# Encoder block on one core: q/k rows in another order, rotary low parts on VectorE, splits at the ends of projections, entry squares on two engines

## The chip, the cores and the metric

One NeuronCore of a Trainium2 chip runs the kernel. It has five engines that run their own instruction lists and wait for each other by semaphores: TensorE (PE in the profile, with PEld for its weight loads), VectorE (DVE), ScalarE (ACT), GpSimd (POOL) and SyncE (SP), which only issues DMA transfers here. DMAs issued by SP, ACT and POOL run on queues of their own. The metric is the device time of one execution in microseconds, the median of several runs.

## What is computed

One encoder block in float32 on an input x of 1024 positions by 1024 features:

```python
h = rms_norm(x, attn_pre_gain[l])
proj = h @ w_in[l]                      # 1024 x 3072
u_hy = proj[..., :3 * HYENA_WIDTH]      # x0, x1, v of the Hyena group, 512 each
q, k, v = jnp.split(proj[..., 3 * HYENA_WIDTH:], 3, axis=-1)
h_fwd, h_bwd = implicit_filters(...)    # small MLP with sines, times a decay window
y_hy = hyena_mixer(u_hy, ...)           # short conv of 3 taps; long conv of v*x1 by FFT; times x0
q = apply_rope(q.reshape(B, S, ATTN_HEADS, 2, ATTN_HEAD_DIM), cos, sin) * scale
k = apply_rope(k.reshape(B, S, ATTN_HEADS, 2, ATTN_HEAD_DIM), cos, sin)
o = differential_attention(q, k, v, lam)   # 4 heads, two softmax maps each, w = p0 - lam * p1
o = rms_norm(o, subln_gain[l], SUBLN_EPS) * (1.0 - lam_init)
mix = jnp.concatenate([y_hy, y_attn], axis=-1) @ w_out[l]
x = x + rms_norm(mix, attn_post_gain[l])
h = rms_norm(x, mlp_pre_gain[l])
y = jnp.square(jax.nn.relu(h @ w_up[l])) @ w_down[l]
x = x + rms_norm(y, mlp_post_gain[l])
```

## The kernel before

**High and low parts.** Every matmul operand is split into a rounded high part (type fp32r) and the rest, its low part, and a product is three matmuls: high by high, high by low, low by high. ACT writes the high part (`act`, a copy), and `less` subtracts it from the full value on POOL ("P") or DVE ("V"), at line L146. `tt` is a tensor_tensor on either of these two engines (L361).

**Buffers.** SBUF tiles come from tagged rings: A 32, B 12, W 6, T 8 and U 6 tiles of 4 KB a partition. A new tile of a tag waits until the oldest one's last reader, a store included, is done. PSUM has banks for single tiles (`bank`) and two double ones for the projections (`bank2`).

**Order of the work, up to the attention.**
- *Entry.* Eight tiles x0 to x7 are loaded. Of the first four, ACT squares each with an accumulated row sum (`square`, L268), `normalize` makes the reciprocal root (L128 to L136) for tiles 0 and 1, for 2, and for 3, and DVE scales them (`xn`, L273). PE transposes them (`n1t`, L278), ACT and DVE make hT's high and low parts (L281, L282), and the projections begin (`pj`, L251).
- *Projections* of 128 columns take 48 matmuls of 512 columns. Those of x1 and v of the Hyena group come first, with a three-tap convolution (`short_conv`, L334 on ACT, L336 on DVE).
- *Filter spectrum*, in two halves of 256 channels (`filter_spectrum`): PE makes `hsp` (L497, L498), DVE multiplies by the decay table `dec` to `hst` (L501), ACT and POOL or DVE split it (`hsd`, L505 and L146; the string EHS names the engines in turn), PE transforms it (L355), and `eight` adds and subtracts the transforms (EWG names the engine of each of nine steps) and stores them to `gd` (L520).
- *The q/k stage.* `todo` has four pairs: (t, pr) with t = 0 for q, 1 for k. A pair has 256 raw columns, 4 heads' parts of 64; it is turned into two streams z = 0, 1 (first and second halves of the rotary dimension), each 128 columns, so `pjqk101` is t = 1, pr = 0, z = 1. `pair_raw` loads, `pair_split` splits, `stream` runs the 48 matmuls. `rotary_a` (after the first stream) makes ac and as, `rotary_b` (after the second) makes bs and bc, adds them to the two turned halves, splits them (ACT and POOL), and stores four tiles of 512 KB to `qk` (L748, two from ACT's queue and two from POOL's).
- *Beside it*, DVE works off `turn_uv` and two `conv_unit`s: the DFT of v times x1 (tiles b0u to b7u, L355), sums and differences (sdeu, ev1u, sdou, opu, nxu, exu), products with the filter spectrum (`unit_product`: loads G0u and G1u, t2, abu, dfu, pq0u, pq1u) and stores. These are generators: `stream` and `vector` keep two estimated times, PE's and DVE's, and a piece of a unit is placed in the order whenever DVE's estimate lies behind PE's.
- *x0.* Four more streams (pj0 to pj3) with their short convolutions, then v, then the attention: scores `s`, DVE's row maximum `nm` (L955), ACT's exponential, and so on. Output projection and MLP follow.

The order is written out by hand (manual scheduling) on all engines in these stages. The pair's columns of high and low weights stand head first, then place in the rotary half:

```python
raws.append(raw.rearrange("p k (g z j) -> p z (k g) j", z=2, j=32))
...
hv, lv = (x[:, 4 * kh:4 * kh + 4, :].rearrange("p k (g j) -> p (k g) j", j=32) for x in (hi, lo))
```

so a tile's 128 rows are 4 heads by 32 places, and the store's outer dimension is (h c), 4.

## Time and profile before

| | us |
|---|---|
| median of 3 runs (lowest, highest) | 1296.97 (1296.13, 1297.72) |
| the profiled execution, its own time | 1294.01 |
| its span, first to last instruction | 1292.2 |
| PE busy | 1217.1 (94%) |
| DVE busy | 1014.6 (79%) |
| ACT busy | 534.5 (41%) |
| POOL busy | 221.3 (17%) |
| mean granted clock of TensorE | 0.982 |

The granted clock is a share of full speed, 2.4 GHz; 0.50 is TensorE's other level, 1.2 GHz. Engines work side by side, so busy shares don't add. An instruction's idle time in square brackets is the time that its engine stood before it, and behind the arrow is what let it go.

### The profile page before, as it was taken

To read this page: it belongs to the slowest core of one execution; us is meant where nothing else is said; L and a number is where in the kernel's file an instruction comes from. 1 tells how busy PE (TensorE), PEld (TensorE's weight loads), DVE (VectorE), ACT (ScalarE), POOL (GpSimd) and SP (SyncE) were. 2 spreads that over 40 slices of the span, in tenths; PEclk is the share of its full clock that TensorE was granted. 3 is DMA by queue.
4 is the path that set the end of the run, shared out by engine and by line. 5 is a ranking of instruction groups with operands and counts; after the bars stand their busy time and mean duration, and the time that the engine had idled before them with its cause. 6 is when DMAs were issued, how large, how long until landed. Compare 5 with 4: busy or idle time off the path is not lost.

```text
span 1292.2 us, 16582 instructions
## 1 busy us (share of the span) xinstructions
PE 1217.1 (94%) x6064; PEld 1018.6 (79%) x6064; DVE 1014.6 (79%) x1698; ACT 534.5 (41%) x1040; POOL 221.3 (17%) x229
## 2 busy tenths in 40 slices
PE   6999899779999999899998999999999999999985
PEld 4787588668989898788886888888887888888873
DVE  5756889897866999956799766687778889887887
ACT  5423231122166777633454323233235544444433
POOL 1233224335131265200100000011110000000000
PEclk9999799889999999999999999999999999999997
DMA  8230424555875342123622432434580704354043
GB/s 253 52 108 16 163 99 131 149 174 186 239 162 123 109 128 68 58 98 101 201 91 74 147 129 91 152 125 157 196 322 10 291 21 162 146 196 163 1 146 115
DMA packets 109720, 172.85 MB, mean 134 GB/s; under 512 B 24587, under 2 KB 71750, under 8 KB 109638
## 3 DMA queue, kind: packets, MB, share of 16 engines
q1 hardware_dynamic: 79334, 125.31, 29.4%
q0 software_dynamic: 29248, 42.28, 11.5%
q10 hardware_dynamic: 1056, 4.19, 1.0%
q8 instruction: 48, 0.79, 0.2%
q14 instruction: 34, 0.28, 0.1%
HBM read 121.10 MB, written 50.33 MB: 133 GB/s over the span
## 4 chain that ended last, share of the span: by engine, by line
PE 68%; DVE 16%; issue 7%; DMA 5%; ACT 2%; POOL 1%; ACTq 0%; DVEq 0%; SPq 0%; POOLq 0%
PE dx L1517 11%; PE pj L251 10%; PE ux L1356 9%; PE mix L1068 7%; PE dz L1517 6%; PE uz L1356 4%; PE s L949 4%; PE o L995 3%; PE dy L1517 3%; PE uy L1356 2%; PE wtp L980 2%; DMA qk<-as 2%; PE v L806 2%; DMA wv_raw<-in_w_in_dram 1%; DVE nm L955 1%
## 5 line engine op out<-in xcount | busy, mean ns | idle before, releaser
L251 PE MATMUL pj<-hT,wi_hi 128*128 128x512 f32 x384 | 124.0, 402 | 0.3 <-DVE hT L282 0.3
L955 DVE TENSOR_REDUCE nm<-s 128x1 f32<-128x1024 f32 x64 | 77.4, 1215 | 31.5 <-PE s L949 31.4
L1517 PE MATMUL dx<-dpT,dpS 128*128 128x512 f32 x384 | 89.2, 390 | 3.7 <-ACT dpT L1500 2.6
L1068 PE MATMUL mix<-wo,yc 128*128 128x512 f32 x384 | 89.8, 392 | 0.0
L251 PE MATMUL pjqk<-hT,wq_hi 128*128 128x512 f32 x256 | 81.7, 401 | 7.4 <-DVE as L697 6.9
L1517 PEld LDWEIGHTS dx<-dpT,dpS 128*128 128x128 f32 x384 | 71.9, 188 | 19.7 <-ACT dpT L1500 3.0
L957 ACT ACTIVATE p<-s,nm 128x1024 f32<-128x1024 f32 x64 | 71.4, 1117 | 38.3 <-DVE nm L955 18.6
L251 PEld LDWEIGHTS pj<-hT,wi_hi 128*128 128x128 f32 x384 | 72.2, 192 | 16.6 <-issue 1.9
L1068 PEld LDWEIGHTS mix<-wo,yc 128*128 128x128 f32 x384 | 71.4, 188 | 14.4
L251 PE MATMUL pj<-hT,wi_lo 128*128 128x512 f32 x192 | 76.7, 400 | 1.2 <-POOL wi_lo L146 1.2
L995 PEld LDWEIGHTS o<-v,wt 128*128 128x128 f32 x512 | 62.1, 191 | 2.6
L995 PE MATMUL o<-v,wt 128*128 128x128 f32 x512 | 62.2, 275 | 0.0
L251 PEld LDWEIGHTS pjqk<-hT,wq_hi 128*128 128x128 f32 x256 | 48.2, 193 | 17.8 <-issue 8.5
L1517 PE MATMUL dx<-dpT,dpA 128*128 128x512 f32 x192 | 48.2, 407 | 4.8 <-ACT dpT L1500 4.1
L251 PE MATMUL pjqk<-hT,wq_lo 128*128 128x512 f32 x128 | 50.8, 397 | 0.0
L1517 PEld LDWEIGHTS dx<-dpT,dpA 128*128 128x128 f32 x192 | 37.2, 195 | 15.4 <-ACT dpT L1500 5.6
L1517 PE MATMUL dy<-dpB,dpA 128*128 128x512 f32 x192 | 46.7, 401 | 2.1 <-ACT dpB L1500 1.5
L1500 ACT ACTIVATE dpA<-dg 128x512 fp32r<-128x512 f32 x48 | 30.1, 628 | 44.5 <-PE dx L1517 26.8
L146 DVE TENSOR_TENSOR wS<-wur,wS 128x512 fp32r<-128x512 f32 x64 | 43.6, 686 | 5.0 <-ACT wS L1349 4.9
L806 PE MATMUL v<-wv_hi,hT 128*128 128x256 f32 x256 | 47.0, 284 | 0.0
L949 PE MATMUL s<-stK,stQ 128*128 128x512 f32 x128 | 42.6, 413 | 4.2 <-ACT p L957 4.2
L1349 ACT ACTIVATE wS<-wur 128x512 fp32r<-128x512 f32 x64 | 37.5, 625 | 21.7 <-DVE wur L1343 15.0
(424 smaller groups left out, 3108.5 us busy)
## 6 DMA issues: line engine op xcount, KB each, us to landing
wur<-in_w_up_dram SPq DMA_DIRECT2D x32, 512.0 KB
dg<-gu SPq DMA_DIRECT2D x32, 512.0 KB
dw<-in_w_down_dram SPq DMA_DIRECT2D x32, 512.0 KB
gu<-gb POOLq DMA_DIRECT2D x16, 512.0 KB, 2.9
wi_raw<-in_w_in_dram SPq DMA_DIRECT2D x12, 512.0 KB
dS<-gs SPq DMA_DIRECT2D x24, 256.0 KB
gu<-ga POOLq DMA_DIRECT2D x10, 512.0 KB, 3.7
x<-in_x_dram SPq DMA_DIRECT2D x8, 512.0 KB
```

The lines of the kernel that those rows point to most:

```text
L146: (G if eng == "P" else V).tensor_tensor(out=out, in0=in_, in1=f32(hi), op=ALU.subtract)
L251: mm(out=pj[c][:, hf * 512:hf * 512 + 512], lhsT=w[:, k, :], rhs=hT[k][s][hf], start=(k == 0 and n == 0), stop=(k == KT - 1 and n == 2))
L806: mm(out=pt[:, col:col + 256], lhsT=hT[k][s][hf][:, q0:q0 + P], rhs=ws[k // 4][o][:, k % 4, :], start=(n == 0), stop=(n == 3 * KT - 1))
L949: mm(out=soft["s", n][e][:, ks], lhsT=stacks[hd, "Q", e][:, qs], rhs=stacks[hd, part, e][:, ks], start=(z == 0), stop=(z == 1))
L955: V.tensor_reduce(out=nmax[:, e:e + 1], in_=soft["s", n][e], axis=AX.X, op=ALU.max, negate=True)
L957: act(out=pc, in_=soft["s", n][e], func=AF.Exp, bias=nmax[:, e:e + 1], accum_out=soft[hd, "r0"][:, qt:qt + 1] if e == 0 else soft["r", n][ ...
L995: mm(out=soft["ov", h][:, i * P:(i + 1) * P], lhsT=wt[:, k // 4, (k % 4) * P:(k % 4) * P + P], rhs=vv[hd // 2, k // 4][:, k % 4, (hd % 2) ...
L1068: mm(out=mixed[i][:, sl], lhsT=ycat[c][hf][s][:, q0:q0 + P], rhs=wo[c][o][:, sl], start=(c == 0 and n == 0), stop=(c == 7 and n == 2))
L1349: act(out=hi, in_=block(p, OVER[n]), func=AF.Copy)
L1356: mm(out=out, lhsT=w[s_][:, k, :], rhs=x[o][k], start=(m in (1, 2, 5) and k == 0 and n == 0), stop=(k == 3 and n == 2), skip_group_check=m ...
L1500: act(out=t[:, 0, :], in_=blk[p, nm], func=AF.Copy)
L1517: mm(out=down_bank(c, m, tp), lhsT=g[s_][:, tp * P:tp * P + P], rhs=w[o], start=(m in (1, 2, 5) and j == 0 and n == 0), stop=(j == PC - 1 ...
```

## The change

- `hsd`'s low parts and all nine steps of `eight` are on DVE (EHS, EWG).
- The gain vector's load moves from SP's queue to POOL's.
- A pair's columns are ordered place first, then head: `pair_split` writes with a step of four elements, the rotary table repeats each place four times, and the stores have an outer dimension of 32.
- In `rotary_b`, both adds come first, then the two low parts on DVE; ACT copies both high parts before it issues its two stores. The planner counts six operations of 1024 columns there, not four.
- The next pair's (or x0's) split stands at the end of the stream; raw weights of x0 are loaded up to two streams ahead.
- At the entry, the second square is a product and a sum on DVE, one normalisation serves four tiles, the fourth tile is scaled by ACT, and the gain columns are made before it.
- The first decay table of a half takes a buffer of tag U. In `conv_unit`, `fetch(1)` and `fetch(3)` come later, filters are loaded one at a time at four places, and ny reuses the tile oc.

```diff
@@ -33,8 +33,8 @@
 
 CONV_LAG = 8.0
 
-EHS = "PV"
-EWG = ("VPPVVVVVV", "PPVVVVVVV")
+EHS = "V"
+EWG = ("VVVVVVVVV", "VVVVVVVVV")
 EWU = ("V" * 9, "V" * 9)
 EUV = "VPVPVPVV"
 ELV = "PP"
@@ -168,7 +168,7 @@
     rows = slot("B", [64, P], F32, "rows")
     V.memset(rows, 0.0)
     gain = slot("B", [8, P], F32, "gain")
-    nc.sync.dma_start(out=gain, in_=a["attn_pre_gain"].rearrange("o (k p) -> (o k) p", p=P))
+    nc.gpsimd.dma_start(out=gain, in_=a["attn_pre_gain"].rearrange("o (k p) -> (o k) p", p=P))
 
     def load_rows():
         nc.sync.dma_start(out=rows[8:44], in_=a["conv_w"].rearrange("o w (k p) -> (o w k) p", p=P))
@@ -228,7 +228,7 @@
         for kh in range(2):
             raw = slot("W", [P, 4, 256], F32, f"wq{t}{pr}{kh}_raw")
             nc.sync.dma_start(out=raw, in_=a["w_in"][0].rearrange("(k p) n -> p k n", p=P)[:, 4 * kh:4 * kh + 4, c0:c0 + 256])
-            raws.append(raw.rearrange("p k (g z j) -> p z (k g) j", z=2, j=32))
+            raws.append(raw.rearrange("p k (g z j) -> p z k g j", z=2, j=32))
         return raws
 
     def pair_split(raws, t, pr, z):
@@ -236,7 +236,7 @@
         hi = slot("W", [P, KT, P], F32R, f"wq{t}{pr}{z}_hi")
         lo = slot("W", [P, KT, P], F32R, f"wq{t}{pr}{z}_lo")
         for kh in range(2):
-            hv, lv = (x[:, 4 * kh:4 * kh + 4, :].rearrange("p k (g j) -> p (k g) j", j=32) for x in (hi, lo))
+            hv, lv = (x[:, 4 * kh:4 * kh + 4, :].rearrange("p k (j g) -> p k g j", g=4) for x in (hi, lo))
             act(out=hv, in_=raws[kh][:, z], func=AF.Copy)
             less("P", lv, raws[kh][:, z], hv)
         wcols["qk", t, pr, z] = hi, lo
@@ -267,9 +267,18 @@
         xn[i] = slot("U" if i < 4 else "B", [P, D], F32, f"xn{i}")
         act(out=xn[i], in_=xs[i], func=AF.Square, accum_out=ssq[:, i:i + 1])
 
-    def normalize(i0, n):
+    def square_v(i):
+
+        xn[i] = slot("U", [P, D], F32, f"xn{i}")
+        V.tensor_tensor(out=xn[i], in0=xs[i], in1=xs[i], op=ALU.mult)
+        V.tensor_reduce(out=ssq[:, i:i + 1], in_=xn[i], axis=AX.X, op=ALU.add)
+
+    def normalize(i0, n, on_act=()):
         r = mean_rstd(ssq[:, i0:i0 + n], n, f"n1_{i0}")
         for i in range(n):
+            if i in on_act:
+                act(out=xn[i0 + i], in_=xs[i0 + i], func=AF.Copy, scale=r[:, i:i + 1])
+                continue
             V.tensor_scalar(out=xn[i0 + i], in0=xs[i0 + i], scalar1=r[:, i:i + 1], scalar2=None, op0=ALU.mult)
 
     def norm1_t(hf, k):
@@ -289,11 +298,12 @@
             load_x(i)
         for c in (5, 9):
             raws[c] = col_raw(a["w_in"][0], c, f"wi{c}", "B")
-        for i0, n in ((0, 2), (2, 1), (3, 1)):
-            for i in range(n):
-                square(i0 + i)
-            normalize(i0, n)
+        square(0)
+        square_v(1)
+        square(2)
+        square(3)
         load_cols(gain, gcols)
+        normalize(0, 4, (3,))
         wcols[4] = col_split(raws[4], "wi4")
         for k in range(KT):
             norm1_t(0, k)
@@ -483,7 +493,7 @@
 
         dec = []
         for i in range(2):
-            t = slot("T", [P, 4, 256], F32, f"dec{hf}_{i}")
+            t = slot("UT"[i], [P, 4, 256], F32, f"dec{hf}_{i}")
             nc.sync.dma_start(out=t, in_=a["c_decay"][4 * i:4 * i + 4, :, hf * 256:hf * 256 + 256].rearrange("t p c -> p t c"))
             dec.append(t)
         fb = slot("T", [1, 256], F32, f"fb{hf}")
@@ -544,13 +554,11 @@
-        def filters(kt):
...
+        gs = {}
+
+        def filters(kt, m):
+            g = gs[kt, m] = slot("T", [P, 2, 2, 256], F32, f"G{m}{nm}{kt}")
+            nc.sync.dma_start(out=g.rearrange("p s c n -> p s (c n)"), in_=g_dram[hf][2 * kt + m])
...
-        fetch(1)
...
+        fetch(1)
         fetch(7, "co")
-        fetch(3)
-        dft_done[0] = hf
...
+            if n == 1 and w == 0:
+                fetch(3)
...
-        gs = filters(0)
+        for m in range(2):
+            filters(0, m)
...
-        gs = filters(1)
...
-        ny = pairs(f"ny{nm}")
+        ny = oc
...
+        if filters:
+            filters(1, 0)
...
@@ -646,6 +656,8 @@
             V.tensor_tensor(out=pq[m][:, 0, :], in0=t[:, 0, :], in1=t[:, 1, :], op=ALU.add)
             yield T512
             V.tensor_tensor(out=pq[m][:, 1, :], in0=t[:, 0, :], in1=t[:, 1, :], op=ALU.subtract)
+            if filters and m == 0:
+                filters(1, 1)
             nc.sync.dma_start(out=q_dram[u][m], in_=pq[m])
             yield T512
 
@@ -738,48 +750,49 @@
         bs, bc = (slot("U", [P, L], F32, f"b{x}{nm}") for x in "sc")
         turned_by(t, bs, pb, rope[1])
         turned_by(t, bc, pb, rope[0])
-        vector(4 * T1024)
-        for z, (x_, y_, op) in enumerate(((ac, bs, SUB), (bc, as_, ADD))):
+        vector(6 * T1024)
+        both = ((ac, bs, SUB), (bc, as_, ADD))
+        for x_, y_, op in both:
             tt("V", x_, x_, y_, op)
+            act(out=y_.bitcast(F32R), in_=x_, func=AF.Copy)
+        for z, (x_, y_, op) in enumerate(both):
             hi, lo = y_.bitcast(F32R), x_.bitcast(F32R)
-            act(out=hi, in_=x_, func=AF.Copy)
-            tt("P", lo, x_, y_, SUB)
+            tt("V", lo, x_, y_, SUB)
             for s_, half in enumerate((hi, lo)):
                 (nc.scalar, nc.gpsimd)[s_].dma_start(
-                    out=qk_dram[t][2 * pr:2 * pr + 2, :, s_, 32 * z:32 * z + 32, :].rearrange("h c j l -> (h c) j l"), in_=f32(half))
+                    out=qk_dram[t][2 * pr:2 * pr + 2, :, s_, 32 * z:32 * z + 32, :].rearrange("h c j l -> j (h c) l"), in_=f32(half))
 
     with tc.manual_schedule(engines=MAN):
         beside += [turn_uv(), conv_unit(0, uv), conv_unit(1, uv)]
         todo = [(t, pr) for pr in range(2) for t in range(2)]
         raws = {todo[0]: pair_raw(*todo[0])}
-        pair_split(raws[todo[0]], *todo[0], 0)
-
-        def next_raw(n):
-            if n < 4:
-                raws[todo[n]] = pair_raw(*todo[n])
-            else:
-                raws[0] = col_raw(a["w_in"][0], 0, "wi0")
-
-        def next_split(n):
-            if n < 4:
-                pair_split(raws[todo[n]], *todo[n], 0)
-            else:
-                wcols[0] = col_split(raws[0], "wi0")
-
-        pair_split(raws[todo[0]], *todo[0], 1)
-        for n, (t, pr) in enumerate(todo):
-            pa = stream(("qk", t, pr, 0), {0: [lambda: next_raw(n + 1)]})
-            ab_ = rotary_a(t, pr, pa)
-            pb = stream(("qk", t, pr, 1), {6: [lambda: next_split(n + 1)]})
-            if n + 1 < 4:
-                pair_split(raws[todo[n + 1]], *todo[n + 1], 1)
-            rotary_b(t, pr, pb, *ab_)
-
-        def x0_next(c):
-            wcols[c] = col_split(col_raw(a["w_in"][0], c, f"wi{c}"), f"wi{c}")
-
+        for z in range(2):
+            pair_split(raws[todo[0]], *todo[0], z)
+
+        def x0_raw(c):
+            raws[c] = col_raw(a["w_in"][0], c, f"wi{c}")
+
+        def x0_split(c):
+            wcols[c] = col_split(raws[c], f"wi{c}")
+
+        for n, u in enumerate(todo):
+            more = todo[n + 1:n + 2]
+            pa = stream(("qk", *u, 0), {0: [lambda: raws.update({w: pair_raw(*w) for w in more}) if more else x0_raw(0)]})
+            for w in more:
+                pair_split(raws[w], *w, 0)
+            if not more:
+                x0_split(0)
+            ab_ = rotary_a(*u, pa)
+            pb = stream(("qk", *u, 1), {} if more else {2: [lambda: x0_raw(1)]})
+            for w in more:
+                pair_split(raws[w], *w, 1)
+            if not more:
+                x0_split(1)
+            rotary_b(*u, pb, *ab_)
         for c in range(4):
-            stream(c, {4: [lambda: x0_next(c + 1)]} if c < 3 else {})
+            stream(c, {2: [lambda: x0_raw(c + 2)]} if c < 2 else {})
+            if c in (0, 1):
+                x0_split(c + 2)
             o = short_conv(c, "U", f"x0_{c}")
             vector(3.0)
             nc.sync.dma_start(out=x0_dram[c], in_=o)
@@ -1777,7 +1790,7 @@
     invf = (f4(10000.0) ** (-np.arange(0, DH, 2, dtype=f4) / f4(DH))).astype(f4)
     ang = (np.arange(L, dtype=f4)[:, None] * invf[None, :]).astype(f4)[tau].T
     co, si = np.cos(ang), np.sin(ang)
-    rope = np.stack([np.concatenate([co] * 4), np.concatenate([si] * 4)]).astype(f4)
+    rope = np.stack([np.repeat(co, 4, axis=0), np.repeat(si, 4, axis=0)]).astype(f4)
     return {"c_fwd": fwd.reshape(4, P, 1024), "c_inv": inv.reshape(4, P, 512), "c_z": zt,
             "c_decay": dec, "c_rope": rope}
 
```

The order moves at three places that matter below. On DVE around the third pair of q/k (`ac01` and `as01` belong to its first stream, `bs10` to the second pair's second), before:

```order
L699 TENSOR_TENSOR bs10_1845<-pjqk101_1768,rope1_1406 128x1024
L699 TENSOR_TENSOR bc10_1846<-pjqk101_1768,rope0_1405 128x1024
L361 TENSOR_TENSOR ac10_1764<-ac10_1764,bs10_1845 128x1024
L361 TENSOR_TENSOR bc10_1846<-bc10_1846,as10_1765 128x1024
...
L634 TENSOR_TENSOR abu00_1903<-nxu0_1762,exu0_1661 128x512
L636 TENSOR_TENSOR abu00_1903<-exu0_1661,nxu0_1762 128x512
L638 TENSOR_TENSOR dfu00_1904<-nxu0_1762,exu0_1661 128x512
...
L646 TENSOR_TENSOR pq0u00_1922<-abu00_1903 128x512
L697 SCALAR_TENSOR_TENSOR ac01_1925<-pjqk010_1863,rope0_1405 128x1024
L697 SCALAR_TENSOR_TENSOR as01_1926<-pjqk010_1863,rope1_1406 128x1024
```

and after the change:

```order
L711 TENSOR_TENSOR bs10_1825<-pjqk101_1756,rope1_1391 128x1024
L711 TENSOR_TENSOR bc10_1826<-pjqk101_1756,rope0_1390 128x1024
L371 TENSOR_TENSOR ac10_1752<-ac10_1752,bs10_1825 128x1024
L371 TENSOR_TENSOR bc10_1826<-bc10_1826,as10_1753 128x1024
L371 TENSOR_TENSOR ac10_1752<-ac10_1752,bs10_1825 128x1024
L371 TENSOR_TENSOR bc10_1826<-bc10_1826,as10_1753 128x1024
...
L709 SCALAR_TENSOR_TENSOR ac01_1904<-pjqk010_1843,rope0_1390 128x1024
L709 SCALAR_TENSOR_TENSOR as01_1905<-pjqk010_1843,rope1_1391 128x1024
L635 TENSOR_TENSOR exu0_1639<-exu0_1639,t21u00_1884 128x2x256
L637 TENSOR_TENSOR exu0_1639<-exu0_1639,t21u00_1884 128x2x256
L644 TENSOR_TENSOR abu00_1934<-nxu0_1779,exu0_1639 128x512
```

The two low parts (the second L371 of ac10 and of bc10) are new on DVE, and the reads of the third pair's first stream now stand ahead of abu, dfu and pq0u. On PE, the first DFT tile of unit 1, b4u1, before:

```order
L251 MATMUL pjqk111_2091<-hT5_1_1_387,wq111_hi_2007 128x512
L251 MATMUL pjqk111_2091<-hT5_1_0_386,wq111_lo_2008 128x512
L355 MATMUL b4u1_2154<-uv0_0_1395,fw2_669 128x256
L355 MATMUL b4u1_2154<-uv0_1_1396,fw2_669 128x256
```

and after the change:

```order
L251 MATMUL pj1_2221<-hT0_1_1_314,wi1_hi_2131 128x512
L251 MATMUL pj1_2221<-hT0_1_0_313,wi1_lo_2133 128x512
L365 MATMUL b4u1_2256<-uv0_0_1380,fw2_654 128x256
L365 MATMUL b4u1_2256<-uv0_1_1381,fw2_654 128x256
```

It stood behind 42 of the 48 matmuls of the last q/k stream; now it stands behind that stream, the whole of pj0 and 27 of pj1. On DVE around the first row maximum of the attention (`nm0_0`), before:

```order
L646 TENSOR_TENSOR pq0u11_2577<-abu11_2570 128x512
L648 TENSOR_TENSOR pq0u11_2577<-abu11_2570 128x512
L646 TENSOR_TENSOR pq1u11_2578<-dfu11_2571 128x512
L648 TENSOR_TENSOR pq1u11_2578<-dfu11_2571 128x512
L955 TENSOR_REDUCE nm0_0_2842<-s0_0_0_2844 128x1
L955 TENSOR_REDUCE nm0_0_2842<-s1_0_0_2845 128x1
```

and after the change:

```order
L968 TENSOR_REDUCE nm0_0_2825<-s0_0_0_2827 128x1
L644 TENSOR_TENSOR abu11_2553<-sdou11_2388,eyu1_2333 128x512
L646 TENSOR_TENSOR abu11_2553<-eyu1_2333,sdou11_2388 128x512
L648 TENSOR_TENSOR dfu11_2554<-sdou11_2388,eyu1_2333 128x512
L650 TENSOR_TENSOR dfu11_2554<-sdou11_2388,eyu1_2333 128x256
L652 TENSOR_TENSOR dfu11_2554<-eyu1_2333,sdou11_2388 128x256
L968 TENSOR_REDUCE nm0_0_2825<-s1_0_0_2828 128x1
L656 TENSOR_TENSOR pq0u11_2560<-abu11_2553 128x512
```

The last sums of unit 1 stood ahead of both maxima; now five of them stand between the two, and pq0u and pq1u behind.

## Rows read from the trace of the kernel before

**Rows 1.** The page: busy time by engine, and the chain by engine.

```profile
PE 1217.1 (94%) x6064; PEld 1018.6 (79%) x6064; DVE 1014.6 (79%) x1698; ACT 534.5 (41%) x1040; POOL 221.3 (17%) x229
...
PE 68%; DVE 16%; issue 7%; DMA 5%; ACT 2%; POOL 1%; ACTq 0%; DVEq 0%; SPq 0%; POOLq 0%
```

**Rows 2.** Busy us (and instructions) of PE, PEld, DVE, ACT, POOL by stretch; clock, DMA.

```profile
0.00:26.00 26.00, 13.19 (x59) 10.42 (x60) 13.49 (x34) 17.47 (x31) 5.43 (x8) 1.00 0.92 291
235.00:285.00 50.00, 33.45 (x144) 27.45 (x143) 45.98 (x53) 5.51 (x7) 13.06 (x8) 0.84 0.59 164
```

**Rows 3.** Timeline of PE: start, us, line, operation, idle before and its releaser.

```profile
168.82 0.41 PE L678 MATMUL uvt<-ident,sc 128*128 128x128 f32 x2 [1.36 <-DVE sdxg L361]
243.22 1.19 PE L251 MATMUL pjqk<-hT,wq_hi 128*128 128x512 f32 x2 [6.94 <-DVE as L697]
281.03 1.19 PE L355 MATMUL b1u<-uv,fw 128*128 128x256 f32 x4 [9.12 <-DVE sdeu L361]
```

**Rows 4.** The columns of rows 2, for stretches at the lower clock.

```profile
146.00:159.00 13.00, 11.03 (x31) 7.26 (x32) 10.18 (x21) 4.98 (x9) 5.87 (x4) 0.50 0.63 234
242.00:248.00 6.00, 4.79 (x11) 3.81 (x12) 5.93 (x11) 0.00 (x0) 0.00 (x0) 0.50 0.77 214
276.00:285.00 9.00, 3.97 (x12) 3.43 (x13) 9.00 (x15) 0.00 (x0) 0.00 (x0) 0.50 0.66 218
```

**Rows 5.** Timeline of DVE in the q/k stage.

```profile
192.79 1.23 DVE L697 SCALAR_TENSOR_TENSOR bs<-pjqk,rope 128x1024 f32<-128x1024 f32 x1 [3.51 <-PE pjqk L251]
...
200.47 3.46 DVE L361 TENSOR_TENSOR opu<-sdou,sdou 128x1024 f32<-128x1024 f32 x1
...
222.59 1.23 DVE L699 TENSOR_TENSOR bc<-pjqk,rope 128x1024 f32<-128x1024 f32 x1 [2.60 <-DMA qk<-as]
223.73 1.22 DVE L361 TENSOR_TENSOR ac<-ac,bs 128x1024 f32<-128x1024 f32 x1
...
240.72 1.21 DVE L697 SCALAR_TENSOR_TENSOR ac<-pjqk,rope 128x1024 f32<-128x1024 f32 x1
...
252.72 1.29 DVE L622 TENSOR_TENSOR t20u<-nyu,G0u 128x512 f32<-128x512 f32 x2 [3.85 <-DMA G0u<-gd]
...
262.62 2.88 DVE L629 TENSOR_TENSOR nyu<-nyu,t20u 128x512 f32<-128x512 f32 x1
```

**Rows 6.** The page: DMA issues, KB each, median us from issue to landing.

```profile
gu<-gb POOLq DMA_DIRECT2D x16, 512.0 KB, 2.9
...
qk<-ac POOLq DMA_DIRECT2D x4, 512.0 KB, 18.0
```

**Rows 7.** Timeline of POOL in the q/k stage.

```profile
193.28 2.55 POOL L146 TENSOR_TENSOR wq_lo<-wq_raw,wq_hi 128x512 fp32r<-128x512 f32 x2 [8.88 <-ACT wq_hi L240]
...
226.17 2.78 POOL L361 TENSOR_TENSOR ac<-ac,bs 128x1024 fp32r<-128x1024 f32 x1 [7.87 <-ACT bs L745]
```

**Rows 8.** The columns of rows 2, from the second stream's end to the first scores.

```profile
193.00:353.00 160.00, 142.21 (x715) 121.35 (x715) 140.84 (x171) 28.52 (x35) 59.93 (x38) 0.95 0.59 172
```

**Rows 9.** DVE at the second filter half; last, all work on hsd (columns of rows 2).

```profile
146.41 1.42 DVE L501 TENSOR_TENSOR hst<-hsp,dec 128x256 f32<-128x256 f32 x4 [1.19 <-DMA dec<-in_c_decay_dram]
149.60 0.42 DVE L501 TENSOR_TENSOR hst<-hsp,dec 128x256 f32<-128x256 f32 x1 [1.77 <-DMA gd<-exg]
...
159.30 1.29 DVE L361 TENSOR_TENSOR sdeg<-b0g,ceg 128x512 f32<-128x512 f32 x2 [0.94 <-ACT ceg L368]
...
163.52 0.69 DVE L361 TENSOR_TENSOR sdog<-b1g,cog 128x512 f32<-128x512 f32 x1 [1.39 <-ACT cog L368]
...
146.00:160.00 14.00, 6.24 (x29) 5.97 (x30) 4.52 (x4) 4.60 (x8) 5.87 (x4) 0.52 0.58 218
```

**Rows 10.** Timeline of DVE at the entry: the scaling of the four tiles.

```profile
8.15 1.42 DVE L273 TENSOR_SCALAR xn<-x,n_r 128x1024 f32<-128x1024 f32 x2
...
11.55 2.80 DVE L273 TENSOR_SCALAR xn<-x,n_r 128x1024 f32<-128x1024 f32 x1
```

**Rows 11.** Timeline of DVE: the first two row maxima of the scores.

```profile
354.69 2.43 DVE L955 TENSOR_REDUCE nm<-s 128x1 f32<-128x1024 f32 x2 [1.72 <-PE s L949]
```

More of the change, by code (lines that the diff above doesn't have):

```diff
@@ L545, in sum_diff_ @@
             return t
-        def filters(kt):
-            out = []
-            for m in range(2):
-                g = slot("T", [P, 2, 2, 256], F32, f"G{m}{nm}{kt}")
-                nc.sync.dma_start(out=g.rearrange("p s c n -> p s (c n)"), in_=g_dram[hf][2 * kt + m])
-                out.append(g)
-            return out
+        gs = {}
+        def filters(kt, m):
+            g = gs[kt, m] = slot("T", [P, 2, 2, 256], F32, f"G{m}{nm}{kt}")
+            nc.sync.dma_start(out=g.rearrange("p s c n -> p s (c n)"), in_=g_dram[hf][2 * kt + m])
         fetch(4, "ce")
@@ L595, in conv_unit @@
             yield T256
-        yield from unit_product(0, hf, (nx, ex), gs)
-        gs = filters(1)
+        yield from unit_product(0, hf, (nx, ex), gs, filters)
         oo = pairs(f"oo{nm}")
@@ L611, in conv_unit, with unit_product @@
                 yield T512
-        yield from unit_product(1, hf, (ny, ey), gs)
-    def unit_product(kt, hf, X, gs):
+        yield from unit_product(1, hf, (ny, ey), gs, None)
+    def unit_product(kt, hf, X, gs, filters):
         u = 2 * kt + hf
@@ L617, in unit_product @@
         for m in range(2):
-            g = gs[m]
+            g = gs[kt, m]
             x = X[m].rearrange("p s (c n) -> p s c n", c=2)
```

## Prediction

> **What bounds the kernel now.** I read the page first: PE is busy 94% of the span and DVE 79%, and the chain that ended last is PE for 68%, DVE for 16% and DMA for 5% [rows 1]. The kernel is therefore as long as PE's work, plus the places where PE stands, plus what PE does at its lower clock. The busy table by stage shows such places [rows 2]: in the first 26 us PE works 13.19, and from 235 to 285 only 33.45 of 50, at a mean clock of 0.84. In that stretch DVE is busy 45.98 of 50, so PE waits for DVE, and the timeline names the waits: 6.94 us before the sixth q/k stream, released by `as` of L697, and 9.12 us before the tile b1u of the second convolution unit, released by `sdeu` [rows 3]. After both waits PE ran at half of its 2.4 GHz: the granted clock is 0.50 from 242 to 248 and from 276 to 285, with 4.79 and 3.97 us of PE work in them [rows 4].
>
> Why is DVE late there? It read the second stream at 192.79, when PE had just ended it, and PE ended the sixth at 236.28 (6.94 before 243.22); so four streams take 43.5 us, 10.9 each, and the one of `ac` at 240.72 had ended at 225.4 [rows 3, 5]. DVE came to it 15 us late, for three reasons. It waits 2.60 us for a store of a q/k tile to land before it may write `bc`. Adds of 512 columns, 0.60 to 0.68 us alone, take up to 2.88 while POOL runs a rotary low part of 2.78 [rows 5, 7]. And its order puts operations of the convolution ahead. Before b1u one more is added: 3.85 us for the load of a filter, G0u [rows 5]. The q/k stores of 512 KB land 18.0 us after their issue, where another of 512 KB from the same queue takes 2.9 [rows 6].
>
> **The change, part by part.** The sum is made against the profiled execution, 1294.01 us with a span of 1292.2; it lies 2.96 us under the median of 1296.97, and that difference is added at the end.
>
> *Order of the q/k stage.* `ac` and `as` of the third pair now stand ahead of abu, dfu and pq0u. I walked DVE's new order with the paces of the rows (1.14 us for 1024 columns, from the starts of two neighbours [rows 5]; 0.60 to 0.64 for 512, from pairs such as 1.28 [rows 9]) from the end of the second stream on: every stream is read within 3 us of its end, and its PSUM tile is wanted again only a stream, 10.9 us, later. So the 6.94 us go, with a margin of 8. The four DFT tiles of unit 1 move behind 81 more matmuls of PE (6 of the last stream, 48 of pj0, 27 of pj1), 18 us at 10.9 us for 48. By the walk DVE frees the first of them 85 us after the second stream, and b1u wants it at 88. The second pair of filter loads is now issued inside the product of the first, as buffers come free, so the 3.85 us are not in the walk. So the 9.12 us go too: 6.94 + 9.12 = **16.1 us**. Without a stop the clock has no cause to fall that these rows show; half of the work done at 0.50 is saved, (4.79 + 3.97) / 2 = **4.4 us** [rows 4].
>
> *Rotary low parts on DVE.* Eight subtractions of 1024 columns at 1.14 add 9.1 us. What goes are the stalls beside POOL's eight: five operations stood there, the first 3.46 us instead of 1.22 and the last 2.88 instead of 0.68 [rows 5]; at 2.2 each that is 11. DVE was busy 140.84 us between 193 and 353 [rows 8]; now some 139.
>
> *Stores divided by 32.* If they land in about 2.9 us, the wait of 2.60 goes. It is no term of its own, since the walk counts on it; if they don't, see the second rival. The loads back into stK, stQ and stk keep their form.
>
> *Splits of the pair weights.* POOL's 16 halves now read raw weights and high parts at a step of four elements, and ACT writes so. The trace of this case has no such access; a half takes 1.27 us now (2.55 for two) [rows 7]. PE would not notice up to about 5 us a half, as two of them have a stream's 10.9 us. DVE would, through its stalls. The ends are nothing and the 2.2 us of the stalls above; I take nothing, as all shapes and counts are the same.
>
> *Splits at the ends of streams.* Weights of the next stream are split while PE has a whole stream, 10.9 us, ahead of it; POOL's two operations of 2.5 us together [rows 7], and ACT's two before them, lie inside. I cost this at nothing; where a raw load or ACT's queue runs late the cover is gone and PE stands, which the edges of the range hold. The fourth x0 stream is the tightest: by the walk 2 us.
>
> *Filter spectrum.* The first decay table is fetched earlier, so the 1.19 us at 146.41 go. The third hst tile still waits for a store of exg, which had landed by 149.60 [rows 9]; with one load of 512 KB fewer ahead of it I take 1.5 us sooner. Against that DVE gets four more low parts and four more adds. Four low parts took it 4.52 us beside POOL's four; eight at 0.60 are 4.8. The adds, 4 x 0.64 = 2.6, fill waits of 0.94 and 1.39 [rows 9]. That is 1.5 - 0.3 + 0.94 + 1.39 - 2.6 = **0.9 us** at PE's next wait, at 168.82 [rows 3]. The slow clock from 146 to 159 [rows 4] gives nothing back while PE waits for DVE anyway. Ends: -1 (the store lands no sooner) and 2.4.
>
> *Entry.* The last `xn` took 2.80 us beside POOL's wi_lo, two others 1.42 together [rows 10], so 2.1 were lost. Now ACT scales the fourth tile, one normalisation serves four, and the second square is DVE's. As one root for all four waits for the last x, and the DMA share was 0.92 [rows 2], I take half: **1.0 us**, ends 0 and 2.6. The gain vector passes from SP's queue, full of loads there, to POOL's, where nothing is ahead of it.
>
> *Attention start, a cost.* Of the 160 us from 193 to 353 about 139.5 are left without the stops, and DVE has 139 of work, with two or three waits for the end of a stream: DVE is as full as PE. Before, it had been done 1.72 us before the first reduction of the scores could start [rows 11]. The new order also lets abu and dfu of the last product run between the first two reductions, 2.7 us. I take **-2 us**; ends 0 and -5.
>
> Sum: 16.1 + 4.4 + 0.9 + 1.0 - 2.0 = 20.4; 1273.6 for the profiled execution, **1276.6** as a median. A measurement of this kernel can tell about 0.2%, 2.6 us, from no change.
>
> **The rivals.**
> 1. *DVE becomes the bound.* For it: 139 us of work in 139.5. Each further microsecond of stall then comes out at the first scores, or at a PSUM tile of the x0 stage. Ten of POOL's 16 halves fall into this stage. Half as long again (0.64) with DVE standing for it costs 6.4 us, and an x0 tile that is freed late another 4: gain 10, about 1287. Against it: not every half has an add of DVE beside it. Chance 0.20. The Trainium skill (GPSIMD Engine Reference, its table of what slows a kernel) says that GpSimd reads at a step above 8 bytes cost about 2.9 cycles an element instead of 1.9, half as much again; by that rule alone the sum would be 14.0 instead of 20.4. No row here shows it.
> 2. *The stores stay slow.* Tag U has six buffers and a pair takes four, so `bs` of the next pair needs one of the last pair's. With 18 us to land, after an issue 8.5 us behind the second stream, it is free at 26.5 and wanted at 21.8: 5 us at each of three pairs on a full DVE, 13 to 15 with the order behind it. Gain 6.4, about 1290. Against it: the 2.9 us [rows 6]. Chance 0.08. The Trainium skill (DMA: Bandwidth & Descriptors, How many engines (k)) spreads a transfer over the largest number up to 16 that divides its slowest dimension, so 4 engines before and 16 now; by that the stores take about a quarter of the 18.0 us, and this rival falls.
> 3. *Slower.* The same halves at a price that only a run can show, with DVE standing beside each of the ten for the whole of the extra time. From 20.4 / 10 = 2.0 us more a half (3.3 instead of 1.27) the gain is gone; at 3.3 more the change loses 13 us, about 1310. For it: DVE did stand 2.2 us beside POOL's operations [rows 5, 7]. Against it: a half has as many elements as now, and not every half meets an add. Chance 0.07.
> 4. *All of it, and more.* No loss at the scores, entry and filter at their best ends, 25.5 us, and some of the half of 11 us of PE work that ran at 0.50 in the filter place [rows 4]: 1266 to 1271. Chance 0.12.
>
> **How the numbers follow.** The forecast has 0.50, the rivals 0.47; 0.03 are left for losses elsewhere that cancel the gain. Faster by over 0.2%: 0.50 + 0.20 + 0.12 and 0.06 of the second rival = 0.88. Slower: 0.07. Same: 0.05. The range runs from the end of the fourth rival, 1266, to the second, 1290; outside are the third and the edges.
>
> **What would show it.** Right: no PE wait over 2 us from 170 to 330 and no 0.50 there; qk stores that land under 6 us; rotary operations within 3 us of a stream's end; first scores near 333. Wrong: POOL halves over 2 us with DVE adds as long beside them; a DVE wait for a qk store; PE waiting at the x0 tiles or the second score tile; or a gap before the second filter half that is as long as before.

## The result and the profile after

| | before | changed | ratio, 95% interval |
|---|---|---|---|
| median, us (4 runs each) | 1296.86 | 1278.66 (1277.97 to 1279.39) | 0.986 [0.9842, 0.9877] |
| span of the profiled execution | 1292.2 | 1276.8 | |

The kernel became 18.2 us faster in medians, and 15.4 us in the two profiled spans: the profiled execution of before, at 1294.01, was 2.85 us under the median of these four (2.96 under that of the three in the table ahead of the change). The page of the changed kernel, its busy line and its chain, beside [rows 1]:

```profile
PE 1216.9 (95%) x6064; PEld 1019.6 (80%) x6064; DVE 1012.2 (79%) x1714; ACT 540.8 (42%) x1037; POOL 182.6 (14%) x207
...
PE 71%; DVE 14%; DMA 1%; ACT 1%; issue 1%; DVEq 0%; ACTq 0%
```

The busy sums are nearly the same but for POOL, which lost 39 us; what changed is where PE stands. DMA's share of the chain fell from 5% to 1%. I read the difference from three marks that both traces have: DVE's read of the second q/k stream (`bs` at 192.79 in [rows 5]), PE's first scores, and PE's first transposes of softmax weights (wtp), which stand just ahead of the scores of the fourth tile; from there on the two kernels take nearly the same time. PE's marks are in the timelines of before and of the changed kernel, and `bs` in that of DVE:

```profile
353.56 0.63 PE L949 MATMUL s<-stK,stQ 128*128 128x512 f32 x2
...
370.31 1.03 PE L980 MATMUL wtp<-ident,p 128*128 128x128 f32 x8
```

```profile
329.64 0.63 PE L962 MATMUL s<-stK,stQ 128*128 128x512 f32 x2
...
354.44 1.04 PE L993 MATMUL wtp<-ident,p 128*128 128x128 f32 x8
```

```profile
192.19 1.23 DVE L709 SCALAR_TENSOR_TENSOR bs<-pjqk,rope 128x1024 f32<-128x1024 f32 x1 [5.04 <-PE pjqk L251]
```

| mark, us | before | changed | gained in the stretch |
|---|---|---|---|
| `bs` of the second stream | 192.79 | 192.19 | 0.60 |
| first scores | 353.56 | 329.64 | 23.32 |
| first transposes, ahead of the fourth tile | 370.31 | 354.44 | -8.05 |
| end of the span | 1292.2 | 1276.8 | -0.47 |

**The middle stretch is full.** In the busy table (columns of [rows 2]), from just behind `bs` to the first scores, beside [rows 8]:

```profile
193.00:329.00 136.00, 136.00 (x712) 117.45 (x711) 118.50 (x163) 32.99 (x35) 41.35 (x30) 1.00 0.60 201
```

PE is busy all of 136 us at a clock of 1.00, so the two long stops of [rows 3] and both slow stretches of [rows 4] are gone. DVE is busy 118.5 of 136, not all of it as I had counted. The stores that [rows 6] showed at 18.0 us (page, DMA issues, KB, us to landing):

```profile
qk<-ac POOLq DMA_DIRECT2D x4, 512.0 KB, 5.3
qk<-bc POOLq DMA_DIRECT2D x4, 512.0 KB, 5.5
```

**The gain of entry and filter is lost again at 179.** The timeline of PE, beside [rows 3]: the wait for the uvt tiles comes 4.26 us sooner, but a new one of 2.48 follows.

```profile
164.56 0.63 PE L690 MATMUL uvt<-ident,sc 128*128 128x128 f32 x4 [1.45 <-DVE sdxg L371]
179.33 0.98 PE L365 MATMUL b0u<-uv,fw 128*128 128x256 f32 x6 [2.48 <-DVE uv L146]
```

DVE and POOL at that place (their timelines), and the clock behind it (busy table):

```profile
172.34 2.88 DVE L371 TENSOR_TENSOR exg<-exg,sdxg 128x256 f32<-128x256 f32 x2
```

```profile
171.48 3.46 POOL L146 TENSOR_TENSOR wq_lo<-wq_raw,wq_hi 128x512 fp32r<-128x512 f32 x2 [39.05 <-ACT wq_hi L240]
```

```profile
180.00:184.00 4.00, 3.78 (x18) 3.37 (x17) 4.00 (x8) 0.58 (x1) 0.00 (x0) 0.64 0.55 221
```

Two adds of 256 columns, 0.75 us elsewhere, stand until POOL's split of the next pair ends; `uv` is 2.1 us later, PE waits, and its clock is 0.64 for the next 4 us.

From the uvt wait to `bs` the changed kernel takes 27.63 us, the kernel before 23.97. Seven traces of this document have the wait for `uv` (1.96 to 2.49 us). In four of them (the kernels below that differ from the changed one at the first scores alone) the clock stayed at 1.00 behind it, and the stretch is 26.1 us, as with tag U:

```profile
180.41 0.98 PE L365 MATMUL b0u<-uv,fw 128*128 128x256 f32 x6 [2.48 <-DVE uv L146]
```

```profile
180.00:184.00 4.00, 3.37 (x22) 3.04 (x23) 4.00 (x8) 0.59 (x1) 0.00 (x0) 1.00 0.33 131
```

So some 2.1 us are the price of the stall, and up to 1.5 more that of the clock where it fell. One trace alone fixes a mark here to some 2 us only: six kernels with the same code up to uvt have it at 164.56 to 166.33, and the changed kernel's is the earliest.

**Eight microseconds are lost at the first scores.** DVE's timeline, beside [rows 11]:

```profile
325.97 1.29 DVE L630 TENSOR_TENSOR t20u<-sdou,G0u 128x512 f32<-128x512 f32 x2 [4.73 <-DMA pq<-pq0u]
...
331.03 5.52 DVE L633 TENSOR_TENSOR eyu<-eyu,G1u 128x512 f32<-128x512 f32 x2
...
337.68 1.21 DVE L968 TENSOR_REDUCE nm<-s 128x1 f32<-128x1024 f32 x1
...
341.28 1.22 DVE L968 TENSOR_REDUCE nm<-s 128x1 f32<-128x1024 f32 x1
```

POOL in the same stretch, and PE, which had its first scores at 329.64:

```profile
330.53 5.47 POOL L146 TENSOR_TENSOR wv_lo<-wv_raw,wv_hi 128x1024 fp32r<-128x1024 f32 x2 [22.08 <-ACT wv_hi L211]
```

```profile
333.27 0.39 PE L819 MATMUL v<-wv_lo,hT 128*128 128x256 f32 x1 [1.39 <-POOL wv_lo L146]
336.05 0.39 PE L819 MATMUL v<-wv_lo,hT 128*128 128x256 f32 x1 [1.08 <-POOL wv_lo L146]
340.18 1.22 PE L962 MATMUL s<-stK,stQ 128*128 128x512 f32 x2 [2.68 <-ACT p L970]
343.79 1.22 PE L962 MATMUL s<-stK,stQ 128*128 128x512 f32 x2 [1.53 <-ACT p L970]
```

Two things delay the first maximum to 337.68, and a third the second. The tile t20u takes a buffer of tag T that the store of pq0u still held (4.73 us); the product eyu stands beside POOL's split of the second v weights (5.52 instead of 1.29); and five sums stand between the two maxima. PE waits 6.68 us in four places, and the scores of the second tile run at the low clock (1.22 us for two, 0.63 at 329.64 in the same operation's row; busy table):

```profile
340.00:346.00 6.00, 4.29 (x10) 3.00 (x11) 6.00 (x12) 1.60 (x5) 2.17 (x3) 0.50 0.86 179
```

### The profile page after: what moved, and what is told of

The parts are those of the page before. It is cut to its first block, busy times and chain, and to the rows that moved or that the text cites. A ratio compares the mean times of both kernels' runs of the same rounds, so it can differ in the third digit from the quotient of the medians.

```text
span 1276.8 us, 16560 instructions
## 1 busy us (share of the span) xinstructions
PE 1216.9 (95%) x6064; PEld 1019.6 (80%) x6064; DVE 1012.2 (79%) x1714; ACT 540.8 (42%) x1037; POOL 182.6 (14%) x207
## 4 chain that ended last, share of the span: by engine, by line
PE 71%; DVE 14%; DMA 1%; ACT 1%; issue 1%; DVEq 0%; ACTq 0%
PE ux L1369 12%; PE dx L1530 11%; PE mix L1081 7%; PE dz L1530 6%; PE uz L1369 6%; PE pjqk L251 6%; PE s L962 4%; PE o L1008 3%; PE pj L251 3%; PE uy L1369 3%; PE dy L1530 3%; PE wtp L993 2%; PE v L819 2%; DVE nm L968 1%; PE iv L899 1%
```

## Experiments

All are edits of the changed kernel, but for the one on the kernel before. Times are medians; each ratio is to runs of the kernel before on the same chip. The last two columns are the stretches of the table above (before: 160.77 and 16.75; changed: 137.45 and 24.80).

| kernel | us | ratio, 95% interval | `bs` | `bs` to first scores | scores to fourth tile |
|---|---|---|---|---|---|
| changed | 1278.66 | 0.986 [0.9842, 0.9877] | 192.19 | 137.45 | 24.80 |
| old rows | 1297.1 | 1.0 [0.9978, 1.0021] | 191.65 | 152.54 | 28.44 |
| rows alone, on the kernel before | 1288.43 | 0.9956 [0.9941, 0.9972] | 191.88 | 153.06 | 18.02 |
| rotary low parts on POOL | 1285.83 | 0.9926 [0.9904, 0.9947] | 192.43 | 143.84 | 24.50 |
| filter work on POOL | 1275.91 | 0.9846 [0.9825, 0.9867] | 188.45 | 137.46 | 25.13 |
| old entry | 1277.15 | 0.9856 [0.9838, 0.9874] | 190.95 | 137.46 | 24.88 |
| old places of the splits | 1276.62 | 0.9839 [0.9808, 0.9871] | 190.01 | 137.46 | 24.06 |
| t2 of the last product in tag U | 1273.82 | 0.9816 [0.9793, 0.9839] | 191.73 | 137.46 | 20.73 |
| second wv_lo on DVE | 1274.07 | 0.9821 [0.9799, 0.9844] | 191.47 | 137.46 | 21.13 |
| both of these | 1275.05 | 0.9832 [0.9803, 0.9861] | 192.44 | 137.46 | 19.65 |
| tag U, v weights early | 1273.56 | 0.9842 [0.9824, 0.9861] | 191.31 | 137.46 | 19.05 |
| tag U, filter work on POOL | 1269.76 | 0.9811 [0.9795, 0.9828] | 188.59 | 137.46 | 19.40 |
| tag U, filter on POOL, v weights early | 1269.85 | 0.979 [0.9763, 0.9818] | 187.94 | 137.46 | 20.92 |

**Old rows.**

```diff
-            raws.append(raw.rearrange("p k (g z j) -> p z k g j", z=2, j=32))
+            raws.append(raw.rearrange("p k (g z j) -> p z (k g) j", z=2, j=32))
-            hv, lv = (x[:, 4 * kh:4 * kh + 4, :].rearrange("p k (j g) -> p k g j", g=4) for x in (hi, lo))
+            hv, lv = (x[:, 4 * kh:4 * kh + 4, :].rearrange("p k (g j) -> p (k g) j", j=32) for x in (hi, lo))
-    rearrange("h c j l -> j (h c) l")
+    rearrange("h c j l -> (h c) j l")
-    rope = np.stack([np.repeat(co, 4, axis=0), np.repeat(si, 4, axis=0)]).astype(f4)
+    rope = np.stack([np.concatenate([co] * 4), np.concatenate([si] * 4)]).astype(f4)
```

> The changed kernel with the pair's rows head first again, so the stores have an outer dimension of 4 and the splits no step of four elements. Theory (the stores' spread carries the q/k stage): q/k stores land in about 18 us again, DVE waits some 5 us for a buffer of tag U at each of three pairs, PE stops again, time 1285 to 1296. Rival A (the stores don't matter once the order is new): landing 18 us, no DVE wait over 1 us, time 1278 to 1280. Rival B (the step of four elements costs more than the stores give): POOL's two halves back from 3.1 to 4.1 us to 2.6, time below 1277.

The whole gain went. Its page and the timelines of DVE and PE:

```profile
qk<-ac POOLq DMA_DIRECT2D x4, 512.0 KB, 18.7
```

```profile
219.86 1.22 DVE L711 TENSOR_TENSOR bc<-pjqk,rope 128x1024 f32<-128x1024 f32 x1 [5.22 <-DMA qk<-as]
273.30 1.23 DVE L711 TENSOR_TENSOR bc<-pjqk,rope 128x1024 f32<-128x1024 f32 x1 [5.12 <-DMA qk<-as]
```

```profile
274.67 0.77 PE L251 MATMUL pj<-hT,wi_hi 128*128 128x512 f32 x1 [5.25 <-DVE bc L711]
```

DVE waits 5 us for a buffer of tag U twice, not at three pairs, and PE stops behind the second. The theory holds in kind. The time is a microsecond above its range, and the interval can't tell it from the kernel before; two of the ten executions took 1289.5 and 1289.7 us, the others 1295.3 to 1299.9.

**Rows alone, on the kernel before**: the same four lines, the other way round, and nothing else.

> The kernel before with nothing but the pair's rows place first, then head (stores divided by 32, rotary table and splits to match). Theory (stores and order are both needed: with the old order the stores' part is DVE's wait of 2.60 us and what follows it): q/k stores land in 5 us, the 2.60 us wait goes, PE still stops for as and for sdeu, time 1288 to 1294. Rival A (the stores alone bring it): both PE stops go or fall under 3 us, time 1277 to 1284. Rival B (the steps of four elements eat it): 1295 or more.

The theory held. The 2.60 us wait is gone, but the old order keeps PE's stops, shorter: 3.98 us for `as` and 6.91 for `sdeu`. So the rows alone gave some 6.9 us by medians (3.6 to 7.6 by the interval), the rest of the change without them nothing, and both together 18.2: most of the gain needs both. No run undoes the order of the q/k stage alone, with the filter loads and the decay table's buffer that moved with it; its part is read from these two runs and the traces.

```profile
239.34 1.16 PE L251 MATMUL pjqk<-hT,wq_hi 128*128 128x512 f32 x2 [3.98 <-DVE as L697]
...
273.49 0.77 PE L355 MATMUL b1u<-uv,fw 128*128 128x256 f32 x2 [6.91 <-DVE sdeu L361]
```

**Rotary low parts on POOL.**

```diff
-            tt("V", lo, x_, y_, SUB)
+            tt("P", lo, x_, y_, SUB)
```

> The changed kernel with the eight rotary low parts on POOL again. Theory (DVE's stalls beside POOL cost more than the work): DVE does 9 us less and stalls 11 us more, and the low parts' stores leave 3 us later; DVE some 2 us later at the first scores, time 1279 to 1284. Rival (DVE's work is what counts): DVE earlier, first scores' maximum earlier than 337, time 1272 to 1277.

1285.83, 7 us over the changed kernel by medians, more than the theory's range. In DVE's timeline an add of 512 columns takes 2.88 and two products 3.48 and more, beside POOL's low parts:

```profile
220.32 2.88 DVE L637 TENSOR_TENSOR nxu<-nxu,t20u 128x512 f32<-128x512 f32 x1
223.13 3.48 DVE L630 TENSOR_TENSOR t21u<-exu,G1u 128x512 f32<-128x512 f32 x2
```

```profile
219.27 3.38 POOL L371 TENSOR_TENSOR ac<-ac,bs 128x1024 fp32r<-128x1024 f32 x1
222.60 2.86 POOL L371 TENSOR_TENSOR bc<-bc,as 128x1024 fp32r<-128x1024 f32 x1
```

PE waits for DVE again (its timeline):

```profile
260.06 0.70 PE L251 MATMUL pj<-hT,wi_hi 128*128 128x512 f32 x2 [2.38 <-DVE as L711]
...
285.66 1.02 PE L365 MATMUL b1u<-uv,fw 128*128 128x256 f32 x6 [1.96 <-DVE sdeu L371]
```

I count in DVE's timelines, from 193 to the first scores, the operations beside a tensor_tensor of POOL that took at least 0.25 us longer than the shortest of their form: 15 here, 26.5 us too long in sum; 15 and 27.4 in the kernel before; 5 and 5.4 in the changed kernel.

**Filter work on POOL, old entry, old places of the splits**, each undone alone:

```diff
-EHS = "V"
+EHS = "PV"
-EWG = ("VVVVVVVVV", "VVVVVVVVV")
+EWG = ("VPPVVVVVV", "PPVVVVVVV")
```

> The changed kernel with the filter spectrum's low parts and adds on POOL as before. Theory: PE's wait for uvt moves from 164.6 to about 167.5, 3 us later, and all behind it with it: time 1280.5 to 1283. Rival (the earlier decay table alone gives that gain): no change, 1278 to 1279.5.

```diff
-        square(0)
-        square_v(1)
-        square(2)
-        square(3)
+        for i0, n in ((0, 2), (2, 1), (3, 1)):
+            for i in range(n):
+                square(i0 + i)
+            normalize(i0, n)
         load_cols(gain, gcols)
-        normalize(0, 4, (3,))
```

> The changed kernel with the old entry: four squares on ACT, three normalisations, all scalings on DVE (the gain vector stays on POOL's queue). Theory: the first transposes start at 14.4 instead of 11.5, PE ends the projections ahead of the filter 1.3 us later, and the time is 1279.5 to 1281. Rival (weights that come by DMA hide it): 1278 to 1279.2, the later stages at the same times.

```diff
-            pa = stream(("qk", *u, 0), {0: [...]})
-            for w in more:
-                pair_split(raws[w], *w, 0)
...
+            pa = stream(("qk", t, pr, 0), {0: [lambda: next_raw(n + 1)]})
+            ab_ = rotary_a(t, pr, pa)
+            pb = stream(("qk", t, pr, 1), {6: [lambda: next_split(n + 1)]})
```

> The changed kernel with the splits of the next weights where they were (in the middle of the second stream, and x0's raw weights one stream ahead). Theory (the place of the splits is hidden, as the prediction costed it): POOL's strided halves only stand beside other operations of DVE, time 1277 to 1281. Rival (the places matter: PE waits for wi_lo in the x0 stage, or DVE's adds of the rotary meet POOL's split): a PE wait of 1 to 3 us for wi_lo or wq_lo, time 1281 to 1286.

None of the three is slower than the changed kernel, and all three ratios overlap its interval. The marks say why: each is ahead at `bs`, by 3.74, 1.24 and 2.18 us, and within 0.8 us as long as it behind that. (Six kernels with the changed one's code up to `bs` have it at 191.31 to 192.44, so 1.24 is little beyond what two traces differ by.) In all three the wait for `uv` near 179 is 0.9 to 1.04 us, not 2.48. In the first two DVE's order has exg behind the rotary's `ac` and `as`, which read PSUM beside POOL's split and kept 1.21 us; in the third POOL's split comes later. With the filter work on POOL (timeline of PE, busy table):

```profile
178.31 0.86 PE L365 MATMUL b6u<-uv,fw 128*128 128x256 f32 x5 [0.90 <-DVE uv L146]
```

```profile
176.00:186.00 10.00, 9.11 (x60) 8.18 (x60) 8.92 (x17) 2.06 (x4) 0.00 (x0) 1.00 0.65 237
```

The same ten microseconds of the changed kernel had 7.30 us of PE at a clock of 0.83. The place of the splits was costed at nothing, and its loss was less than the times can tell: 1276.62 lies 0.4 us under the theory's range, and its rival fell. The theories for the entry and for the filter fell.

**The first scores.**

```diff
-            t2 = slot("T", [P, 2, 2, 256], F32, f"t2{m}{nm}")
+            t2 = slot("U" if kt and hf else "T", [P, 2, 2, 256], F32, f"t2{m}{nm}")
```

> The changed kernel with the last product's two tiles t20u and t21u taken from tag U, not T. Theory (DVE's lateness at the first scores comes in part from its wait of 4.73 us for the store of pq0u): the wait goes, the last product ends before or beside POOL's wv_lo, the first maximum comes at 332 to 335 instead of 337.7, time 1272 to 1277. Rival A (POOL's wv_lo stalls DVE whatever stands there): the stall of some 4 us moves to another operation, the first maximum 1 us earlier, time 1277 to 1279. Rival B (tag U is held there by stores of x0): a wait of the same size for another DMA, time 1278 to 1281.

The wait for pq0u's store is gone and the first maximum comes at 330.32. The stall beside POOL moved to the sums between the maxima, as the second half of its rival said, but 4.07 us of the stretch came back:

```profile
330.32 1.22 DVE L968 TENSOR_REDUCE nm<-s 128x1 f32<-128x1024 f32 x1 [2.08 <-PE s L962]
331.46 2.83 DVE L644 TENSOR_TENSOR abu<-sdou,eyu 128x512 f32<-128x512 f32 x1
334.22 2.86 DVE L646 TENSOR_TENSOR abu<-eyu,sdou 128x512 f32<-128x512 f32 x1
...
338.27 1.21 DVE L968 TENSOR_REDUCE nm<-s 128x1 f32<-128x1024 f32 x1
```

```diff
-ELV = "PP"
+ELV = "PV"
```

> The changed kernel with the low parts of the second v weights on DVE, not POOL (ELV PV). Theory (the 5.47 us of POOL at 330.5 hold DVE and PE): DVE has 2.3 us more work and 4.2 us less stall, PE's waits of 1.39 and 1.08 us for wv_lo become waits for DVE; the first maximum at 334 to 337, time 1274 to 1278. Rival (v's weights then wait in DVE's line and PE stops for longer): time 1279 to 1284.

3.67 us came back; PE then waits 3.95 us for DVE's second wv_lo.

> Both: t20u and t21u of the last product in tag U, and the second v weights' low parts on DVE. Theory: no wait over 1 us between 320 and 345 on DVE but for PE's scores, the first maximum at 331 to 334, and 6 to 8 of the 8.5 us come back that are lost between the first scores and the end: time 1270 to 1275. Rival: one of the two is worth nothing by itself, and the time is that of the better one.

With both edits 5.15 us of the stretch, not 7.7, and the time is no better than with one: the theory that they add fell. PE waits 3.12 us for wv_lo, whose raw weights land late: ACT's first copy of them waits 3.58 us for the load, until 328.51.

```diff
-    wv = [v_weights(0)]
+    wv = [v_weights(0), v_weights(1)]
...
-    wv.append(v_weights(1))
```

> The changed kernel with t20u and t21u of the last product in tag U, and the second v weights loaded and split with the first ones, ahead of the first v matmuls, instead of behind them. Theory (at the first scores DVE and PE are held by wv_lo on POOL, whose raw weights land late, near 328): POOL's two wv_lo run before 325, PE does not wait for wv_lo, the second reduction is not behind a stall, and the time is 1269 to 1272.5. Rival (the loads earlier collide with the loads of the stacks, or POOL's queue is held): first scores later than 331 or a new wait for stk, time 1273 to 1280.

With the tag's edit too. POOL's split ran at 290.78 and no wait for wv_lo is left; the stretch is 1.68 us shorter than with the tag alone, yet the time did not move. It lies in the rival's range, but neither of the rival's reasons came: first scores at 328.77, no wait for stk. What is left in the traces of DVE and PE is the second maximum behind abu and dfu:

```profile
331.49 1.22 DVE L967 TENSOR_REDUCE nm<-s 128x1 f32<-128x1024 f32 x1
...
335.16 1.21 DVE L967 TENSOR_REDUCE nm<-s 128x1 f32<-128x1024 f32 x1
```

```profile
337.72 0.50 PE L961 MATMUL s<-stK,stQ 128*128 128x512 f32 x1 [2.52 <-ACT p L969]
```

**Tag U with the filter work on POOL, and all three edits.**

> The changed kernel with t20u and t21u of the last product in tag U and the filter spectrum's low parts and adds on POOL as before. Theory (the filter part of the change costs some 3 us, since DVE then stands at the second uv tiles beside POOL's split and PE's clock falls; it adds to the other gain): first scores near 326, time 1269 to 1272. Rival (both gains end in the same slack of the first scores): as with the tag alone, 1273 to 1275.

> The changed kernel with three edits: t20u and t21u of the last product in tag U, the filter spectrum's low parts and adds on POOL as before, and the second v weights loaded and split ahead of the first v matmuls. Theory (each takes away a stall of its own: the clock's fall at the second uv tiles, the wait for the store of pq0u, wv_lo on POOL): what the last step took from 1273.8, nothing clear, it takes here too, and the time is 1268 to 1270; what is left is the second reduction behind abu and dfu. Rival (with unit 1 done sooner the early v weights save the 2 us stall at abu): 1265 to 1268.

1269.76 and 1269.85: the gains at 179 and at the first scores lie in different stretches (188.59 at `bs`, 19.40 behind the scores) and add. The earlier v weights change nothing here either. These are the best versions that ran, 0.9811 [0.9795, 0.9828] and 0.979 [0.9763, 0.9818] of the kernel before. The order of abu and dfu between the maxima was not tried otherwise.

## Why the prediction was right, and where it was not

The time, 1278.66, is 2.1 us from the 1276.6 of the prediction and inside its range. The terms are less near than the sum, and part of the nearness is luck: between the two profiled executions, on which the sum was made, 15.4 us were gained, not 20.4, and an error of 6 us at the attention start is half hidden by one of 3 the other way in the q/k stage.

- *Order of the q/k stage and the clock: 20.5 forecast, 23.3 measured.* Right in mechanism: both stops and both slow stretches went, and the stretch has no PE gap. It was too small, since I counted the two named stops (16.1) where PE stood 17.8 of the 160 us in [rows 8], and 4.4 for the clock where 5.5 are left for it. (The wait of 6.94 us stands before the seventh stream, not the sixth as the prediction has it at one place; the sum doesn't hang on it.) The length 137.46 appears in every kernel that has fast stores and the low parts on DVE: it is PE's own work.
- *Stores:* "It is no term of its own" was right only in the sum. The second rival's condition, put in by the old rows, gave no gain at all where the rival said 6.4: I counted 13 to 15 us at three pairs, it cost 18 with waits at two. The landing fell from 18.0 to 5.3 us. The Trainium skill (DMA: Bandwidth & Descriptors, How many engines (k)) has a transfer spread over the largest number up to 16 that divides the slowest dimensions of both its sides (here 4 and 128 before, 32 and 128 now), so 4 before and 16 now; the ratio of 3.4 in landing time agrees with that, though a landing holds more than the transfer itself.
- *Low parts on DVE:* stalls of 11 against 9.1 of work, 2 us, was too small a price for the other way: on POOL they cost 6.4 us of the stretch. The term was mis-sized: I counted the five stalls beside low parts, 11 us, and left those beside POOL's splits of weights as they were. By the count above 22 us went, from 27.4 to 5.4, and 21 come back with the low parts on POOL.
- *"DVE is as full as PE"* was wrong. DVE had 118.5 of 136 us, with some 9 us of unit 1's last product left behind the first scores: some 128 where I had 139, the 11 us of stalls that I had not counted as going. So the first rival, DVE as the bound of this stage, had nothing to decide up to the first scores: PE never waited in it. Behind them DVE was late all the same, through waits of its own.
- *Splits at a step of four elements: "I take nothing".* POOL's halves rose from 1.28 to 1.54 us at the least, ACT's from 0.62 to 1.15. My reading of the edit was too wide: in the diff the place j is the last dimension of the raw weights' view before and after, so they are read as before, and only the read of the high part and the write of the low part have the step. The tile views of the changed kernel, and of the old rows:

```profile
L240 ACT ACTIVATE wq_hi<-wq_raw x16: 1122/1145/1180, 108.7 to 236.5; 128x512 fp32r<-128x512 f32 x16
L146 POOL TENSOR_TENSOR wq_lo<-wq_raw,wq_hi x16: 1536/1580/2576, 109.9 to 238.3; 128x512 fp32r<-128x512 f32 x16
```

```profile
L240 ACT ACTIVATE wq_hi<-wq_raw x16: 614/622/636, 108.7 to 235.5; 128x512 fp32r<-128x512 f32 x16
L146 POOL TENSOR_TENSOR wq_lo<-wq_raw,wq_hi x16: 1283/1298/2012, 109.4 to 237.0; 128x512 fp32r<-128x512 f32 x16
```

  (Columns: shortest, median and longest in ns, first and last start.) The Trainium skill (GPSIMD Engine Reference, its table of what slows a kernel) says half as much again for such reads; the row, with one such read of two and such a write, has a fifth, so the measurement decides. The price that rivals one and three took from these halves falls with it: for the gain to go, a half had to take 2.0 us more, and it took 0.25.
- *Filter and entry: 1.9 forecast, 0.6 measured.* Up to the uvt wait more came than was worked out, 4.26 us against 1.9 (2.5 by the latest of the six kernels with this code). But not as worked out: with the filter work on POOL, uvt starts at 164.46, no later than in the changed kernel, so that work on DVE gave nothing; with the old entry it starts at 166.97, 0.6 to 2.4 later. What the earlier decay table gave was not tried by itself. The step that failed stood nowhere in the sum: the work behind that wait, where DVE's exg now meets POOL's split.
- *Attention start: "I take -2 us; ends 0 and -5"; measured -8.05.* The place was right, and so were abu and dfu between the maxima. Missing were the wait for a buffer that pq0u's store held and the stall beside wv_lo, both outside the walk. The two edits give back 4.07 and 3.67 us of it. The shortest stretch that ran, with tag U and the v weights early, is 19.05, 2.30 over the kernel before: near the -2 that I took and the 2.7 of abu and dfu in it, though no run moved these sums.

Of the signs of being right, the stores under 6 us and the rotary reads within 3 us of a stream's end came, and the first scores came sooner than 333; "no PE wait over 2 us from 170 to 330 and no 0.50 there" did not, at 179. Two signs of being wrong came: PE waited at the second score tile, and at two places a half of POOL over 2 us (2.58 and 2.56) stood beside an add as long, here the first in DVE's timeline, without a wait of PE behind it:

```profile
195.82 2.59 DVE L371 TENSOR_TENSOR bc<-bc,as 128x1024 f32<-128x1024 f32 x1
```

## What to carry to other kernels

A wait that is removed shows what stood under it: cost the next stage with its buffers, its loads and its engines' neighbours, not only the order of its operations. Where a store holds a buffer of a small ring, look at its outer dimension before moving work: here 32 instead of 4 took the landing from 18.0 to 5.3 us. Where DVE adds from SBUF to SBUF beside a POOL operation, count the add until POOL's operation ends, or let DVE read PSUM there.
